# Decayed keys of a chunked delta-rule scan: transposes of scaled keys in place of products with diagonal matrices

## The chip, the cores and the metric

The kernel runs on one core of a Trainium2 chip. The metric is the device time of one execution in microseconds (us); the median of several runs is compared. A profiled execution gives the trace from which all rows below come. TensorE is called PE in the trace (its weight loads PEld), VectorE DVE, ScalarE ACT, GpSimd POOL, SyncE SP.

## The reference

A trunk of two residual layers over 512 tokens with 1024 features. Layer 0 mixes tokens by a chunked gating MLP, layer 1 by RWKV-7 time mixing; each is followed by a gated ConvFFN. The change is in the time mixing, whose core is a recurrence per head (16 heads of 64):

```python
def wkv7_scan(r, w, k, v, a, b):
    def step(state, inp):
        r_t, w_t, k_t, v_t, a_t, b_t = inp
        sa = jnp.einsum('bhvk,bhk->bhv', state, a_t)
        state = (state * w_t[:, :, None, :]
                 + sa[..., None] * b_t[:, :, None, :]
                 + v_t[..., None] * k_t[:, :, None, :])
        y_t = jnp.einsum('bhvk,bhk->bhv', state, r_t)
        return state, y_t
    ...
```

with `w` the decay, `a = -kk` and `b = kk * a_h` for normalized keys `kk`.

## The kernel before

The recurrence is done in chunks of 64 tokens (`C = 64`, `NCH = 8` chunks). Two heads share the 128 partitions (`H[0]` is partitions 0 to 63, `H[1]` 64 to 127), so there are eight pairs of heads. For each pair three generators run: `decay` (decays and their inverses; `gc` is the decay over a whole chunk, one number per feature and chunk), `operands` (`ar`: queries and `a` with decays on; `bk`: `b` and `k` with inverse decays on, 128 columns per chunk, and for the second head a copy of `b` at columns 128 to 191), and `products`, which the change edits. It does, for two groups of four chunks (`U = 4`), the products of `bk` with `ar` into the PSUM tiles `aux` (first head) and `us` (second head), masks them on VectorE into `lq`, copies the inner triangle to `ti` on ScalarE and writes `lq` to DRAM (`std`). Then it makes `bt`, the keys turned to have tokens on partitions and decayed to the end of the chunk, for which VectorE builds diagonal matrices `dg` from the identity `id2` and `gc`, and TensorE multiplies `bk` by them. `bt` goes to DRAM (`btd`), from where the scan reads it.

`acc(tag)` takes one of two PSUM buffers of a tag; the tags are `mm`, `aux`, `e` and `us`. `pairs` runs the eight pairs one after the other with the next pair's `operands` and the `decay` of the one after that between; `weave` puts steps of a `fill` generator (dense projections, `L315` to `L317` in the trace) and of `invert(0)` (inversion of the first 4 pairs' triangles: 62 small VectorE instructions, then small matmuls L1025 and L1028) between them. A scheduler below the program orders the instructions of each engine by readiness as it estimates it; engines then run their queues in that order. After the stage the scan over chunks begins (L1186 to L1213), with `invert(1)` on VectorE (from L993 on) beside it. An fp32 matmul shows as two instructions in the trace.

Lines that the text names: L853, L855, L877, L885 matmuls of `decay`; L822, L837 matmuls of the values; L1239 the transposes of the scan's results; L1188 and L1199 the scan's next steps after L1186.

Of the kernel before, what the change touches and what calls it, by code (L numbers as in the profile page):

```python
# [15 lines left out]
ALU = mybir.AluOpType  # L16
# [4 lines left out]
P = 128  # L21
# [4 lines left out]
C = 64  # L26
NCH = T // C
# [117 lines left out]
class Emit:  # L145
# [579 lines left out]
    def rwkv_main(self, r, ctx, gain):  # L725
        nc, tc, A = self.nc, self.tc, self.A
        V, S, G = nc.vector, nc.scalar, nc.gpsimd
        h0, h1 = slice(0, 64), slice(64, 128)
        H = (h0, h1)
        std, btd, vtd, rt, gc, dq = r.std, r.btd, r.vtd, r.rt, r.gc, r.dq  # L730
        U = 4
# [4 lines left out]
        def tile_(shape, tag, bufs):  # L736
            return ep.tile(shape, F32, tag=tag, bufs=bufs, name=self.uid(tag))
# [7 lines left out]
        def bc(t, n):  # L745
            return t.unsqueeze(2).to_broadcast([t.shape[0], t.shape[1], n])
# [167 lines left out]
        def products(p, u):  # L914


            g, i = divmod(p, 4)
            ar, bk = u.ar, u.bk

            dg = tile_([P, NCH, C], "dg", 1)  # L920
            V.tensor_tensor(dg, self.c("id2", C).unsqueeze(1).to_broadcast([P, NCH, C]), bc(gc[:, p], C), ALU.mult)
            masks = self.c("masks", P)

            for ch in (slice(0, U), slice(U, NCH)):
                qs = [self.acc(tag).rearrange("p (c t) -> p c t", t=P) for tag in ("aux", "us")]
                for c in range(ch.start, ch.stop):
                    for hd in range(2):
                        nc.tensor.matmul(qs[hd][:, c - ch.start, :], bk[H[hd], c, C * hd:C * hd + P], ar[H[hd], c, :],  # L928
                                         start=True, stop=True)
                lq = tile_([P, U, 2, P], "lq", 2)  # L930
                for hd in range(2):
                    V.tensor_tensor(lq[:, :, 1 - hd], qs[hd], masks.unsqueeze(1).to_broadcast([P, U, P]), ALU.mult)
                    S.copy(ti[g][H[hd], i, ch], lq[H[hd], :, 1 - hd, 0:C])
                f = lq.rearrange("p c a t -> p c (a t)")
                for hd, o, n, q in ((0, P, P, 0), (0, 2 * P, C, P + C), (1, 0, P + C, C)):
                    nc.sync.dma_start(std[g][ch, H[hd], i, o:o + n].rearrange("c p t -> p c t"), f[H[hd], :, q:q + n])
                yield
            bt = tile_([P, NCH, 2, C], "bt", BT)
            qs = [self.acc(tag).rearrange("p (c t) -> p c t", t=C) for tag in ("aux", "us")]
            for c in range(NCH):  # L940
                for hd in range(2):
                    nc.tensor.matmul(qs[hd][:, c, :], bk[H[hd], c, C * hd:C * hd + P], dg[H[hd], c, :],  # L942
                                     start=True, stop=True)
            for hd in range(2):
                S.copy(bt[:, :, hd, :], qs[hd])
            nc.sync.dma_start(btd[:, :, p].rearrange("c p a t -> p c (a t)"), bt.rearrange("p c a t -> p c (a t)"))
            yield

        def pairs():

            units = [type("Unit", (), {})() for _ in range(KT)]

            def start(p):
                if p >= KT:
                    return iter(())
                while p not in ks:
                    next(fill)
                if p == 0:
                    second_factors(p)
                return decay(p, units[p])  # L960

            yield from start(0)
            nxt = start(1)
            operands(0, units[0])
            for _ in nxt:
                yield
            for p in range(KT):
                nxt = start(p + 2)
                if p + 1 < KT:
                    operands(p + 1, units[p + 1])  # L970
                for _ in products(p, units[p]):
                    next(nxt, None)
                    yield
                done.add(p)
# [411 lines left out]
```

## Time and profile before

| | |
|---|---|
| median of 3 runs | 1292.31 us (1291.89 to 1294.6) |
| profiled execution | 1294.26 us, its span 1292.4 us |
| mean granted TensorE clock | 0.988 |
| TensorE busy | 1269.4 us (98%) |
| VectorE, ScalarE busy | 852.8 us, 631.3 us |
| stage of `products` | from about 602 to 737 us of the span |

Rows of the windows view give the stretch, its length and busy times of PE, PEld, DVE, ACT, POOL with instruction counts, then granted clock, DMA share and GB/s. Rows of the timeline give start, duration, engine, line, operation, output<-inputs, and the count when equal instructions are merged; a matmul's end is modelled, so its cost is read from the start of the next one. Rows of the groups view give the count, total busy time, mean ns of one, and idle time before them with what ended it.

### The profile page before, as it was taken

How to read it: one execution, taken by the hardware profiler on the slowest of the kernel's cores; microseconds unless marked ns; L12 is line 12 of the kernel's file. 1: busy time of each engine (PE TensorE's matmuls, PEld its weight loads, DVE VectorE, ACT ScalarE, POOL GpSimd, SP SyncE). 2: the span in 40 equal slices, each digit the busy share in tenths (PEclk: the TensorE clock that was granted, in tenths of full speed). 3: DMA queues.
4: the chain of work that ended last, by engine and by line, in shares of the span. 5: the costliest groups of instructions: out<-in, count | busy, mean ns of one | idle time of the engine just before them, and what ended most of it. 6: DMA issues, size and time to landing. Idle time of an engine off the chain costs nothing.

```text
span 1292.4 us, 19533 instructions
## 1 busy us (share of the span) xinstructions
PE 1269.4 (98%) x7591; PEld 1018.9 (79%) x7591; DVE 852.8 (66%) x1401; ACT 631.3 (49%) x1084; POOL 97.7 (8%) x119
## 2 busy tenths in 40 slices
PE   9999999999999999999999998999999999999997
PEld 6878888888888888787777776677888888888886
DVE  6465468888886444765889587765677777763233
ACT  5534456555554333565785645532544444442222
POOL 4100100000000000000000022231100000000001
PEclk9999999999999999999999998999999999999998
DMA  7332457777557764236878699764233333333332
GB/s 252 102 98 83 129 172 256 245 245 242 175 171 220 217 206 151 90 106 185 224 199 239 171 215 227 193 168 144 78 104 98 98 97 96 93 93 98 90 90 78
DMA packets 115452, 201.65 MB, mean 156 GB/s; under 512 B 21600, under 2 KB 53600, under 8 KB 115360
## 3 DMA queue, kind: packets, MB, share of 16 engines
q10 hardware_dynamic: 39104, 112.87, 29.0%
q1 hardware_dynamic: 76256, 87.54, 23.4%
q8 instruction: 59, 0.97, 0.3%
q14 instruction: 33, 0.27, 0.1%
HBM read 152.93 MB, written 47.45 MB: 155 GB/s over the span
## 4 chain that ended last, share of the span: by engine, by line
PE 88%; DVE 5%; ACT 1%; POOL 0%; issue 0%; DMA 0%; DVEq 0%; ACTq 0%; POOLq 0%
PE mm L315 10%; PE mm L316 9%; PE mm L317 9%; PE aux L315 6%; PE aux L317 6%; PE aux L316 6%; PE e L316 6%; PE e L315 6%; PE e L317 5%; PE us L317 5%; PE us L315 5%; PE us L316 5%; PE aux L928 1%; PE aux L942 1%; PE us L1186 1%; PE us L1199 1%
## 5 line engine op out<-in xcount | busy, mean ns | idle before, releaser
L234 ACT CAST w<-w 128x512 fp32r<-128x512 f32 x340 | 206.3, 610 | 374.3 <-PE aux L317 94.8
L235 DVE TENSOR_TENSOR w<-w,w 128x512 fp32r<-128x512 f32 x340 | 233.3, 688 | 196.7 <-ACT w L234 196.2
L315 PE MATMUL mm<-mxh,w 128*128 128x512 f32 (+1 forms) x416 | 171.7, 414 | 1.6 <-ACT mxh L234 1.6
L316 PE MATMUL mm<-mxl,w 128*128 128x512 f32 (+1 forms) x416 | 166.7, 401 | 0.2 <-DVE mxl L235 0.2
L317 PE MATMUL mm<-mxh,w 128*128 128x512 f32 (+1 forms) x416 | 166.3, 400 | 0.0
L342 POOL TENSOR_TENSOR ss<-ss,sq 128x512 f32<-128x512 f32 x30 | 41.0, 1368 | 777.6 <-issue 595.1
L315 PEld LDWEIGHTS mm<-mxh,w 128*128 128x128 f32 (+1 forms) x416 | 78.2, 189 | 22.0 <-issue 3.3
L317 PEld LDWEIGHTS mm<-mxh,w 128*128 128x128 f32 (+1 forms) x416 | 78.7, 189 | 18.1 <-issue 1.2
L316 PEld LDWEIGHTS mm<-mxl,w 128*128 128x128 f32 (+1 forms) x416 | 78.9, 190 | 16.3 <-issue 1.1
L539 ACT ACTIVATE cv<-z,par 128x512 f32<-128x512 f32 x88 | 71.7, 817 | 28.8 <-DVE z L537 23.8
L315 PE MATMUL us<-mxh,w 128*128 128x512 f32 x216 | 84.6, 392 | 0.0
L315 PE MATMUL aux<-mxh,w 128*128 128x512 f32 x216 | 84.5, 391 | 0.0
L317 PE MATMUL aux<-mxh,w 128*128 128x512 f32 x216 | 84.2, 390 | 0.3 <-DVE w L235 0.3
L316 PE MATMUL aux<-mxl,w 128*128 128x512 f32 x216 | 84.1, 389 | 0.0
L316 PE MATMUL us<-mxl,w 128*128 128x512 f32 x216 | 84.1, 389 | 0.0
L317 PE MATMUL us<-mxh,w 128*128 128x512 f32 x216 | 84.1, 389 | 0.0
L315 PE MATMUL e<-mxh,w 128*128 128x512 f32 x208 | 81.5, 392 | 2.5 <-ACT mxh L234 2.4
L316 PE MATMUL e<-mxl,w 128*128 128x512 f32 x208 | 81.2, 390 | 0.1
L317 PE MATMUL e<-mxh,w 128*128 128x512 f32 x208 | 81.0, 389 | 0.0
L540 DVE SCALAR_TENSOR_TENSOR cv<-z,par,cv 128x512 f32<-128x512 f32 x88 | 66.1, 752 | 19.9 <-ACT cv L539 19.9
L541 DVE SCALAR_TENSOR_TENSOR cv<-z,par,cv 128x512 f32<-128x512 f32 x88 | 66.0, 752 | 2.9
L315 PEld LDWEIGHTS e<-mxh,w 128*128 128x128 f32 x208 | 39.1, 188 | 11.3 <-ACT mxh L234 3.3
(1088 smaller groups left out, 2605.1 us busy)
## 6 DMA issues: line engine op xcount, KB each, us to landing
w<-in_wup ACTq DMA_DIRECT2D x88, 512.0 KB, 3.7
w<-in_wdn ACTq DMA_DIRECT2D x32, 512.0 KB, 3.6
st<-std SPq DMA_DIRECT2D x30, 320.0 KB, 6.9
w<-wkd ACTq DMA_DIRECT2D x16, 512.0 KB, 5.0
w<-wvd ACTq DMA_DIRECT2D x16, 512.0 KB, 5.7
w<-wod ACTq DMA_DIRECT2D x16, 512.0 KB, 4.3
w<-in_wdn ACTq DMA_DIRECT2D x16, 384.0 KB, 3.4
w<-in_wsu ACTq DMA_DIRECT2D x8, 512.0 KB, 3.7
```

What stands on the lines that cost most here:

```text
L234: nc.scalar.copy(hi[r, :n], src)
L235: (lo_eng or nc.vector).tensor_tensor(lo[r, :n], src, hi[r, :n].bitcast(F32), ALU.subtract)
L315: mm(acc, wh, xh, start=first, stop=False)
L316: mm(acc, wh, xl, start=False, stop=False)
L317: mm(acc, wl, xh, start=False, stop=last)
L342: nc.gpsimd.tensor_tensor(self.ss, self.ss, self.sq, ALU.add)
L539: nc.scalar.activation(c, z[:, 2:], AF.Identity, scale=cw(2, i), bias=self.p("conv_b", l * 44 + i))
L540: nc.vector.scalar_tensor_tensor(c, z[:, 1:T + 1], cw(1, i), c, ALU.mult, ALU.add)
L541: nc.vector.scalar_tensor_tensor(c, z[:, 0:T], cw(0, i), c, ALU.mult, ALU.add)
L928: nc.tensor.matmul(qs[hd][:, c - ch.start, :], bk[H[hd], c, C * hd:C * hd + P], ar[H[hd], c, :], start=True, stop=True)
L942: nc.tensor.matmul(qs[hd][:, c, :], bk[H[hd], c, C * hd:C * hd + P], dg[H[hd], c, :], start=True, stop=True)
L1186: nc.tensor.matmul(us[H[hd], 0, i, :], ar(i, hd, 0), vu[:, hd, i, :], start=True, stop=True)
```

## The change

`dg` goes away. `decayed` multiplies the keys `bk` of four chunks by `gc` on VectorE into `be` (one buffer), and ScalarE copies the second head's 64 columns behind them. `turned` transposes `be` on TensorE (identity `id2`), one transpose per chunk and head, into two PSUM tiles `qb` that are taken after the products of the first chunk group and held until they are copied to `bt`. The first half of the chunks is turned after the first group's products, the second half after the second group's.

```diff
-            dg = tile_([P, NCH, C], "dg", 1)
-            V.tensor_tensor(dg, self.c("id2", C).unsqueeze(1).to_broadcast([P, NCH, C]), bc(gc[:, p], C), ALU.mult)
+            id2, qb = self.c("id2", C), []
+
+            def decayed(ch):
+
+                be = tile_([P, U, 3 * C], "be", 1)
+                V.tensor_tensor(be[:, :, 0:P], bk[:, ch, 0:P], bc(gc[:, p, ch], P), ALU.mult)
+                S.copy(be[h1, :, P:], be[h1, :, 0:C])
+                return be
+
+            def turned(ch, be):
+                for c in range(U):
+                    for hd in range(2):
+                        nc.tensor.transpose(qb[hd][:, ch.start + c, :], be[H[hd], c, C * hd:C * hd + P], id2[H[hd]])
+
+            be = decayed(slice(0, U))
             masks = self.c("masks", P)
 
             for ch in (slice(0, U), slice(U, NCH)):
...
-                yield
+                if not qb:
+                    qb[:] = [self.acc(tag).rearrange("p (c t) -> p c t", t=C) for tag in ("aux", "us")]
+                    turned(ch, be)
+                    be = decayed(slice(U, NCH))
+                yield
+            turned(slice(U, NCH), be)
             bt = tile_([P, NCH, 2, C], "bt", BT)
-            qs = [self.acc(tag).rearrange("p (c t) -> p c t", t=C) for tag in ("aux", "us")]
-            for c in range(NCH):
-                for hd in range(2):
-                    nc.tensor.matmul(qs[hd][:, c, :], bk[H[hd], c, C * hd:C * hd + P], dg[H[hd], c, :],
-                                     start=True, stop=True)
             for hd in range(2):
-                S.copy(bt[:, :, hd, :], qs[hd])
+                S.copy(bt[:, :, hd, :], qb[hd])
```

The scheduler makes a new order of it. In the order of the changed kernel L931 is the transpose, L940 the product (L928 before), L1040 the second step of the inversion (L1028 before), L1198 and L1202 the scan's first matmuls (L1186 and L1190 before). A row stands for one matmul of the program, or for several if a count ends it.

TensorE, first pair, after the products of the second chunk group. Before, the products with `dg` alternate between `aux` and `us`, eight of each (the first two are shown; L877 belongs to `decay`):

```order
L316 MATMUL mm_5072<-mxl_4839,w_854_5018 128x512
L877 MATMUL e_5170<-cst,sq_5162 128x2 x4
L317 MATMUL mm_5072<-mxh_4838,w_854_5018 128x512
L942 MATMUL aux_5187<-dg_5098,bk_4984 128x64
L942 MATMUL us_5188<-dg_5098,bk_4984 128x64
```

In the changed kernel, same engine and place, the transposes of the second half of the chunks:

```order
L317 MATMUL mm_5072<-mxh_4838,w_854_5018 128x512
L931 MATMUL aux_5119<-cst,be_5129 128x64 x4
L315 MATMUL mm_5221<-mxh_4759,w_863_5073 128x512
L316 MATMUL mm_5221<-mxl_4760,w_863_5073 128x512
L317 MATMUL mm_5221<-mxh_4759,w_863_5073 128x512
L931 MATMUL us_5120<-cst,be_5129 128x64 x4
```

Four transposes of one half now stand together, with dense matmuls between them and the four of the other half.

TensorE, fifth pair, its first chunk group (the `decay` matmuls of a later pair are L877, L885, L853, L855). Before:

```order
L928 MATMUL aux_5784<-ar_5578,bk_5583 128x128
L928 MATMUL us_5785<-ar_5578,bk_5583 128x128
L928 MATMUL aux_5784<-ar_5578,bk_5583 128x128
L885 MATMUL e_5737<-cst,n_999_5693 64x128 x8
L928 MATMUL us_5785<-ar_5578,bk_5583 128x128
```

Changed:

```order
L940 MATMUL aux_5801<-ar_5590,bk_5595 128x128 x4
L940 MATMUL us_5802<-ar_5590,bk_5595 128x128 x4
L877 MATMUL e_5714<-cst,sq_5706 128x2 x4
L931 MATMUL aux_5819<-cst,be_5798 128x64 x4
L885 MATMUL e_5753<-cst,n_1005_5719 64x128 x8
L853 MATMUL e_5832<-lr_4357,l_984_5643 128x512
L855 MATMUL e_5832<-lr_4357,l_986_5645 128x512
L940 MATMUL aux_5868<-ar_5590,bk_5595 128x128
```

The products' halves no longer alternate: four of `aux`, then four of `us`; and the first of the second chunk group follows the transposes.

TensorE, from the end of the first inversion to the scan. Before, the second step of the inversion (L1028), from its second quarter to its last, has matmuls of the values (L822) and dense rows between its pieces:

```order
L1028 MATMUL aux_6489<-li_6306,tt_6309 32x32 x16
L822 MATMUL mm_6577<-cst,v_6506 128x128 x2
L1028 MATMUL aux_6559<-li_6306,tt_6309 32x32 x16
L822 MATMUL mm_6577<-cst,v_6506 128x128 x2
L315 MATMUL mm_6508<-mxh_5515,w_1107_6334 128x512
L316 MATMUL mm_6508<-mxl_5516,w_1107_6334 128x512
L317 MATMUL mm_6508<-mxh_5515,w_1107_6334 128x512
L315 MATMUL mm_6508<-mxh_5559,w_1107_6334 128x512
L316 MATMUL mm_6508<-mxl_5560,w_1107_6334 128x512
L317 MATMUL mm_6508<-mxh_5559,w_1107_6334 128x512
L1028 MATMUL aux_6559<-li_6306,tt_6309 32x32 x16
```

Changed:

```order
L1037 MATMUL aux_6441<-ix_6333,ti_4860 32x32 x31
L940 MATMUL aux_6495<-ar_6190,bk_6195 128x128 x4
L1037 MATMUL aux_6441<-ix_6333,ti_4860 32x32
L316 MATMUL mm_6550<-mxl_5680,w_1115_6364 128x512
L317 MATMUL mm_6550<-mxh_5679,w_1115_6364 128x512
L315 MATMUL mm_6550<-mxh_5731,w_1115_6364 128x512
L316 MATMUL mm_6550<-mxl_5732,w_1115_6364 128x512
L1040 MATMUL aux_6531<-li_6334,tt_6337 32x32 x32
L1040 MATMUL aux_6591<-li_6334,tt_6337 32x32 x32
L317 MATMUL mm_6550<-mxh_5731,w_1115_6364 128x512
L1198 MATMUL us_6689<-rb_6481,mxh_6476 64x64 x2
```

The last row is the scan's first. Before, twelve dense rows and L837 stand between the last L1028 and the scan's first L1186; now it is one dense row. The inversion's second step stands in one piece, and the last pair's last products (L940) stand inside its first step (L1037, which was L1025).

## The prediction

> **What bounds the kernel now.** I read the page's first section, then the windows of the stage in which the edited function runs (598 to 742 us), then the waits of TensorE there.
>
> ```profile
> PE 1269.4 (98%) x7591; PEld 1018.9 (79%) x7591; DVE 852.8 (66%) x1401; ACT 631.3 (49%) x1084; POOL 97.7 (8%) x119
> 598.00:742.00 144.00, 143.33 (x1247) 111.63 (x1247) 114.30 (x221) 96.40 (x185) 1.28 (x8) 0.97 0.76 211
> PE aux L1025 <- DVE ix L1010: 0.5, 1, 0.5
> ```
>
> The second line is the stage: length, busy time of PE, PEld, VectorE, ScalarE and GpSimd, then the granted clock. TensorE is busy for 143.33 of 144 us and waits once, for 0.5 us. So the stage ends when TensorE's queue ends: what is taken off TensorE is gained, what is put on it is lost. VectorE (114.30) and ScalarE (96.40) have some room. Behind the stage it is otherwise:
>
> ```profile
> 692.00:700.00 8.00, 8.00 (x62) 6.68 (x60) 6.58 (x16) 5.43 (x13) 0.00 (x0) 0.79 0.53 160
> 736.00:748.00 12.00, 12.00 (x130) 9.73 (x130) 1.91 (x1) 7.21 (x13) 2.36 (x4) 0.58 0.59 143
> 784.00:800.00 16.00, 12.41 (x238) 8.82 (x238) 15.07 (x34) 8.51 (x17) 4.22 (x6) 0.98 0.97 208
> ```
>
> From 784 to 800 VectorE is the full engine (15.07 of 16) and TensorE has holes of 3.6 us: there the second inversion on VectorE decides. The first two lines show the granted clock at 0.79 over 8 us and 0.58 over 12 us, behind long runs of small matmuls: 8 x 0.21 = 1.7 us and 12 x 0.42 = 5.0 us of clock lost.
>
> **The prices on TensorE.** These come from four places of the timeline. First a row of dense matmuls with one half of the products of a chunk group between them:
>
> ```profile
> 719.00 0.40 PE L315 MATMUL mm<-mxh,w 128*128 128x512 f32 x1
> 719.24 0.39 PE L316 MATMUL mm<-mxl,w 128*128 128x512 f32 x1
> 719.46 0.40 PE L317 MATMUL mm<-mxh,w 128*128 128x512 f32 x1
> 719.79 1.16 PE L928 MATMUL us<-ar,bk 64*128 64x128 f32 x8
> 720.88 0.50 PE L315 MATMUL mm<-mxh,w 128*128 128x512 f32 x1
> ```
>
> Dense matmuls start 0.23 us apart, so that is what a row costs. The eight passes of one half (four fp32 matmuls show as eight instructions) push the next dense one from 719.69 to 720.88: 1.19 us. A pass takes (1.16 - 0.27)/7 = 0.127 us, so the edge is 1.19 - 8 x 0.127 = 0.17 us. Now both halves alternating, aux from partitions 0 to 63 and us from 64 to 127:
>
> ```profile
> 611.99 0.39 PE L317 MATMUL mm<-mxh,w 128*128 128x512 f32 x1
> ...
> 613.19 0.27 PE L928 MATMUL aux<-ar,bk 64*128 64x128 f32 x1
> 613.20 0.27 PE L928 MATMUL us<-ar,bk 64*128 64x128 f32 x1
> 613.40 0.50 PE L315 MATMUL mm<-mxh,w 128*128 128x512 f32 x1
> ```
>
> Sixteen passes cost 613.40 - 611.99 - 0.23 = 1.18 us, as much as eight alone: the two halves run side by side only when they alternate in the queue. Then the products with diagonals that go away:
>
> ```profile
> L942 PE MATMUL us<-dg,bk 64*128 64x64 f32 x128 | 16.5, 275 | 0.0
> 615.47 0.48 PE L317 MATMUL mm<-mxh,w 128*128 128x512 f32 x1
> ...
> 617.61 0.27 PE L942 MATMUL us<-dg,bk 64*128 64x64 f32 x1
> 617.81 0.51 PE L315 MATMUL mm<-mxh,w 128*128 128x512 f32 x1
> ```
>
> 32 passes alternating cost 617.81 - 615.47 - 0.23 = 2.11 us for a pair of heads. Seven of the eight pairs alternate wholly or nearly; in the last the halves stand apart, some 32 x 0.127 = 4.1 us. Total: 7 x 2.11 + 4.1 = 18.9 us. The nearest thing to the new transposes:
>
> ```profile
> L1239 PE MATMUL aux<-cst,y 128*128 128x128 f32 x32 | 5.1, 283 | 0.8 <-DVE y L1235 0.8
> 773.09 0.50 PE L315 MATMUL mm<-mxh,w 128*128 128x512 f32 x1
> 773.43 0.60 PE L1239 MATMUL aux<-cst,y 128*128 128x128 f32 x4
> 773.78 0.48 PE L316 MATMUL mm<-mxl,w 128*128 128x512 f32 x1
> ```
>
> A transpose is one instruction, not two (32 for 32 in the code; the 64 products per half show as 128). Four cost 773.78 - 773.09 - 0.23 = 0.46 us, (0.60 - 0.27)/3 = 0.11 us each: a pass of a transpose is no quicker than a pass of a product.
>
> **The change, part by part.**
>
> *Products with diagonals out, transposes in.* In the new queue 13 of the 16 chunk groups have their transposes as four of one half and, later, four of the other; only three groups alternate. A half group of four costs 0.46 us by the full-height row; by the half-height row it is 4 x 0.11 plus an edge of 0.17 to 0.31, up to 0.75 us. I take 0.6 us, since the tile is 64 high as in L928, and no edge for about ten that stand beside other half-height work: 26 x 0.6 - 10 x 0.17 = 13.9. Three alternating groups at 8 x 0.055 + 0.3 = 0.74 add 2.2. Sum 16.1 against 18.9: 2.8 us gained (between 5.4 gained, at 0.46 and 0.5, and 2.8 lost, at 0.75 everywhere).
>
> [...]
>
> *Products of chunk groups.* The accumulators of the transposes are now held from the first chunk group to the end of the pair. Of two buffers for each of aux and us, one is left for the products, so the second chunk group waits for the mask multiplications of the first on VectorE. In the queue this shows as products of which the halves no longer alternate: eight groups of 16 stand apart, where before there were two (of the last pair). Each costs 2 x 1.19 - 1.18 = 1.2 us more when both halves stand alone, about 0.85 when they follow each other (16 x 0.127 - 1.18). 6 x 0.9 = 5.4 us lost (5.1 to 7.2).
>
> *VectorE and ScalarE.*
>
> ```profile
> L921 DVE TENSOR_TENSOR dg<-cst,gc 128x512 f32<-128x512 f32 x8 | 5.5, 687 | 2.9 <-PE us L942 2.9
> L933 ACT COPY ti<-lq 64x256 f32<-64x256 f32 x32 | 12.9, 403 | 10.8 <-DVE lq L932 10.4
> ```
>
> Eight products of 512 columns become sixteen: 8 x 0.69 = 5.5 us more on VectorE. Sixteen copies of 64x256 are added on ScalarE: 16 x 0.40 = 6.5 us. Their cover is the room shown above, 30 and 48 us, and the dense matmuls queued between; queued behind a scaling that waits for its one buffer is the next pair's normalization, for which TensorE would wait. I charge 0.3 us (0 to 5.5, rival D). DMAs are the same in number, size and queue; GpSimd's queue keeps its order, and in SyncE's only some writes of `lq` change places with each other.
>
> *The hand-over to the scan.* Last, the first step of the scan moves up in TensorE's queue. Before, twelve dense rows and L837 stand between the last matmul of the first inversion and L1186; after, one dense row.
>
> ```profile
> 743.72 0.80 PE L315 MATMUL mm<-mxh,w 128*128 128x512 f32 x1
> 743.84 0.58 ACT L1037 COPY ti<-aux 32x512 f32<-32x512 f32 x1 [0.94 <-PE aux L1028]
> 745.02 1.04 ACT L995 COPY ix<-ti 32x1024 f32<-32x1024 f32 x1
> 746.09 2.14 DVE L996 STREAM_TRANSPOSE li<-ix 128x1024 f32<-128x1024 f32 x1 [10.86 <-ACT ix L995]
> 749.61 0.34 PE L1186 MATMUL us<-rb,mxh 128*64 128x64 f32 x4
> 750.34 0.42 DVE L1188 COPY wt<-us 128x256 f32<-128x256 f32 x1
> ```
>
> The dense row at 743.72 is the first behind the inversion, 5.9 us ahead of L1186, in part at half clock. The second inversion begins with L996, 3.5 us ahead of L1186. After, the last products' masks and copies come only some 4 us ahead of L1186, and L996 behind them stands ahead of L1188 on VectorE. So the inversion starts about level with the scan, up to 3.5 to 4 us later against it, and the first L1199 waits about 1 us for L1188. VectorE decides at 784 to 800, so this comes out at the end but for its own idle time of that stretch. Between 0 (all absorbed) and 4, I take 2 us.
>
> *Sum.* -2.8 + 5.4 + 0.3 + 2.0 = 4.9 us. The profiled execution took 1294.26 us (span 1292.4), 1.95 above the median of 1292.31, so I add the sum to the median: 1297.2.
>
> **The rivals.**
>
> *A. The terms cancel (chance 0.24).* Half groups at 0.46 us and the later inversion absorbed: -5.4 + 5.4 + 0.3 = 0.3, so 1292.6 us. For it: the row of L1239 itself. Against it: it is a full-height tile, and half-height bursts show an edge.
>
> *B. Faster by the clock (0.15).* The last pair's products, 4.1 us of small matmuls in the run that ends in the 0.58 clock, are gone, and the transposes in their place lie between dense rows. If neither drop comes, 6.7 us are regained: 4.9 - 6.7 = -1.8; with half groups at 0.46 (3 us less) -4.8, 1287.5 us. It decides from 7.5 us below my sum on. Against it: after the change all 64 second-step matmuls of the inversion still stand in one piece just ahead of the scan's small ones, and around the fifth and the sixth pair runs of products, transposes and L877 of some 5 us form anew.
>
> *C. Slower by the clock (0.06).* If transposes keep the clock down, each further low stretch like that at 692 costs 1.7 us; two more give 1300.6. [...]
>
> *D. VectorE holds TensorE (0.10).* With one buffer left, each second chunk group waits for two mask multiplications in a queue that also carries the scalings. If each is late by one of those, 0.7 us x 8 = 5.5 us more: 1302.7. For it: this dependency is new. Against it: in the stage VectorE waited for TensorE (2.9 us at L921 alone), and TensorE for VectorE only 0.5 us.
>
> **How the numbers follow.** My own case has 0.45: 1297.2, by itself 1295 to 1300. A change within 0.2% (2.6 us) is about what a measurement cannot tell from none. Slower: 0.45 + 0.06 + 0.10 = 0.61; same: 0.24; faster: 0.15. The range reaches from 1290.5, inside B, to 1302.5, just short of D.
>
> **What the profile after would show.** Transposes as 128 instructions in place of 256, 0.11 us apart in fours; products in runs of eight of one half, at 1.19 us each. PE busy in the stage up by 2 to 4 us. L996 starting at about the time of L1186 or later, and holes of TensorE near 790 to 800 larger than 3.6 us. I am wrong if halves that follow each other overlap all the same, if a half group costs below 0.4 us, or if the clock rows at 692 and 736 go to 1.00.

## The result and the profile after

The changed kernel took 1306.4 us (median of 4 runs, 1305.61 to 1310.54) against 1292.1 for the kernel before on the same chip (1291.35 to 1294.6): a ratio of 1.0108, 95% interval 1.0092 to 1.0124. It is 14 us slower; forecast were 4.9. The profiled execution after has a span of 1304.7 us, 12.3 more than before.

Some kernels below spread over 9 to 18 us between executions, and one profile then stands for one execution, not for the median; where the profile lies at one end of the spread, that is said.

By landmarks of the two traces: the products begin 1.1 us later (603.9 against 602.8, already so before the stage), the scan 6.4 later (756.0 against 749.6), its first transposes (L1251 after, L1239 before) 12.3 later (785.7 against 773.4); from there on the distance stays. So 5.3 us are lost among the pairs and 5.9 in the first 30 us of the scan. Busy time hardly tells: TensorE is busy for 1277.4 us (before 1269.4) in 128 fewer instructions.

```profile
PE 1277.4 (98%) x7463; PEld 1018.9 (78%) x7463; DVE 858.7 (66%) x1409; ACT 638.0 (49%) x1100; POOL 97.3 (7%) x119
```

A busy row at half clock counts as busy (704 to 712 below: 8.00 of 8 us busy at a clock of 0.50). The windows view tells the two apart (length, busy PE, PEld, DVE, ACT, POOL, then the granted clock, DMA share, GB/s); first the stage by the times of before, then the places that stand out:

```profile
598.00:742.00 144.00, 140.88 (x892) 104.14 (x890) 116.02 (x224) 92.84 (x183) 1.29 (x8) 0.93 0.73 202
664.00:672.00 8.00, 7.06 (x47) 5.50 (x46) 7.00 (x13) 6.21 (x13) 0.11 (x1) 0.74 0.61 169
672.00:680.00 8.00, 8.00 (x22) 5.57 (x22) 4.44 (x8) 5.29 (x9) 0.00 (x0) 0.62 1.03 305
696.00:704.00 8.00, 6.18 (x39) 4.41 (x37) 7.40 (x17) 6.24 (x13) 0.00 (x0) 0.88 0.38 96
704.00:712.00 8.00, 8.00 (x27) 6.83 (x27) 6.42 (x16) 2.97 (x6) 0.00 (x0) 0.50 0.70 193
752.00:760.00 8.00, 5.80 (x172) 4.45 (x170) 4.29 (x6) 6.72 (x11) 2.35 (x4) 1.00 0.76 173
760.00:768.00 8.00, 7.88 (x69) 5.38 (x67) 6.35 (x21) 3.59 (x8) 1.08 (x2) 0.79 1.06 243
800.00:808.00 8.00, 4.85 (x96) 3.54 (x96) 7.14 (x16) 1.76 (x5) 3.21 (x5) 0.99 1.00 242
808.00:816.00 8.00, 7.62 (x128) 5.05 (x124) 4.59 (x9) 6.33 (x8) 1.24 (x2) 0.50 1.05 247
816.00:824.00 8.00, 7.81 (x146) 5.71 (x146) 4.89 (x10) 5.38 (x11) 2.45 (x3) 0.87 0.25 72
```

Before, at the places of the new drops and behind the second inversion:

```profile
664.00:672.00 8.00, 8.00 (x54) 5.55 (x51) 6.09 (x11) 5.17 (x10) 0.11 (x1) 1.00 0.83 236
672.00:680.00 8.00, 8.00 (x73) 6.83 (x74) 6.30 (x10) 7.88 (x13) 0.00 (x0) 1.00 0.79 209
704.00:712.00 8.00, 8.00 (x60) 6.29 (x60) 7.96 (x19) 4.94 (x12) 0.61 (x2) 1.00 0.97 291
760.00:768.00 8.00, 8.00 (x99) 5.43 (x98) 7.60 (x18) 4.98 (x10) 1.29 (x2) 1.00 1.06 270
800.00:808.00 8.00, 7.82 (x132) 5.56 (x126) 2.69 (x5) 5.67 (x9) 0.80 (x2) 0.61 0.99 219
```

The drop of the clock at 736 to 748 is gone, the one behind the second inversion (before at 800, now at 808) is longer, and three are new or larger: 664 to 680, 696 to 712 and 760. The first new one, in the timeline:

```profile
664.06 0.40 PE L317 MATMUL mm<-mxh,w 128*128 128x512 f32 x1
664.38 1.16 PE L940 MATMUL aux<-ar,bk 64*128 64x128 f32 x8
666.11 1.16 PE L940 MATMUL us<-ar,bk 64*128 64x128 f32 x8 [0.57 <-DVE lq L944]
667.20 1.28 PE L877 MATMUL e<-cst,sq 128*128 128x2 f32 x8
668.43 0.69 PE L931 MATMUL aux<-cst,be 64*128 64x64 f32 x4
669.48 1.98 PE L885 MATMUL e<-cst,n 128*64 128x128 f32 x16 [0.37 <-DVE n L880]
671.39 0.80 PE L853 MATMUL e<-lr,l 128*128 128x512 f32 x1
672.11 0.79 PE L855 MATMUL e<-lr,l 64*128 64x512 f32 x1
672.70 0.62 PE L940 MATMUL aux<-ar,bk 64*128 64x128 f32 x2
673.26 0.79 PE L315 MATMUL mm<-mxh,w 128*128 128x512 f32 x1
```

Between the dense rows at 664.06 and 673.26 stand 9.2 us of other matmuls, nearly all small (L853 and L855 of `decay`, 512 columns wide, come at the end), halves apart, with two short waits. From about L931 on matmuls take longer; the dense row behind takes 0.79 instead of 0.39. I call such a stretch a *piece*: TensorE's queue between two dense rows of the projections.

The parts are sized by windows of 4 us from 590 to 870. *Idle* is the sum of (4 - busy PE), *clock* the sum of 4 x (1 - granted clock), *ahead* the shift of the first L853 at 587, *work* what is left of the change of the span. *Apart* counts, of the 256 product passes, those in rows of four or more of one half, whatever stands between them. These are from one profile each, and *span* to *work* are differences to before, in us. *Lost, all* is not: it is the span times (1 - mean granted clock) over the whole kernel, as a mean over all executions (each clock is known to a thousandth, 1.3 us).

| kernel | median | span | ahead | idle | clock | work | apart | lost, all |
|---|---|---|---|---|---|---|---|---|
| before | 1292.1 | 1292.4 | | (6.9) | (10.2) | | 33 | 13.6 to 14.8 on four chips |
| after | 1306.4 | +12.3 | +1.1 | +4.5 | +6.8 | -0.2 | 126 | 22.2 |
| e1, keys scaled in place | 1309.7 | +14.1 | 0.0 | +9.9 | +8.5 | -4.2 | 53 | 24.3 |
| e2, diagonals, held | 1292.7 | -4.8 | -1.2 | +2.9 | -6.8 | +0.3 | 33 | 12.9 |
| e4, VectorE's columns | 1298.6 | +4.6 | +1.2 | +7.0 | +3.4 | -7.1 | 84 | 19.2 |
| e6, no scaling | 1297.2 | +1.3 | -2.2 | +9.0 | +1.7 | -7.2 | 71 | 18.7 |
| e10, products by identity | 1311.7 | +19.4 | -0.3 | +5.9 | +3.4 | +10.4 | 90 | 16.8 |
| e11, dense rows in pairs 5, 6 | 1301.0 | -0.1 | -1.4 | +2.2 | -6.8 | +5.9 | 80 | 13.3 |
| e12, TensorE's queue as after | 1305.3 | +10.5 | -1.4 | +7.0 | +5.1 | -0.2 | 126 | 20.4 |

After and e12, with the same queue on TensorE, give the same work (-0.2 twice), so that column holds to some tenths. Read: the change made TensorE's work no smaller, and added 6.8 us of lost clock and 4.5 of waiting. The last column bears the clock out beyond one profile: some 8 us more are lost than before. A us of lost clock is not quite a us of time: within the seven kernels that were executed twelve times the time rises by 0.7 to 1.0 us with it.

### The profile page after: what moved, and what is told of

Read it like the earlier page. It is cut to its first block, busy times and chain, and to the rows that moved or that the text cites. A ratio compares the mean times of both kernels' runs of the same rounds, so it can differ in the third digit from the quotient of the medians.

```text
span 1304.7 us, 19309 instructions
## 1 busy us (share of the span) xinstructions
PE 1277.4 (98%) x7463; PEld 1018.9 (78%) x7463; DVE 858.7 (66%) x1409; ACT 638.0 (49%) x1100; POOL 97.3 (7%) x119
## 4 chain that ended last, share of the span: by engine, by line
PE 87%; DVE 5%; ACT 2%; issue 1%; POOL 0%; DVEq 0%; ACTq 0%; POOLq 0%
PE mm L315 10%; PE mm L317 9%; PE mm L316 9%; PE aux L315 6%; PE aux L317 6%; PE aux L316 6%; PE e L316 5%; PE e L315 5%; PE e L317 5%; PE us L317 5%; PE us L315 5%; PE us L316 5%; PE aux L940 1%; PE e L885 1%; PE us L1198 1%; PE us L1211 1%
```

## The experiments

All kernels are made from the changed one, but for e8, e13 and e15, made from the kernel before. In brackets behind a time stand its ratio to the kernel before on the same chip and the 95% interval.

**First question: why do the halves stand apart?** The prediction blamed the accumulators that are held. e1 holds none; e2 holds them, but multiplies with diagonals; e4 moves the second head's columns from ScalarE to VectorE; e5 is e1 with e4's edit.

```diff
 e1: in the loop, instead of `be`; transposes of bk and self.acc behind the loop
+                V.tensor_tensor(bk[:, ch, 0:P], bk[:, ch, 0:P], bc(gc[:, p, ch], P), ALU.mult)
+                S.copy(bk[h1, ch, P:], bk[h1, ch, 0:C])
 e2: dg as before the change, in turned():
-                        nc.tensor.transpose(qb[hd][:, ch.start + c, :], be[...], id2[H[hd]])
+                        nc.tensor.matmul(qb[hd][:, c, :], bk[...], dg[H[hd], c, :], start=True, stop=True)
 e4 (e5 the same on bk):
-                S.copy(be[h1, :, P:], be[h1, :, 0:C])
+                V.tensor_tensor(be[h1, :, P:], bk[h1, ch, P:], bc(gc[h1, p, ch], C), ALU.mult)
```

> The same transposes and the same ScalarE copy as in the changed kernel, but the keys are scaled in place after the products of their chunk group, and both accumulators are taken only after the second group, as before the change: none is held across the groups. Before is about 1292 us, after about 1306. T1 (the accumulators held from the first chunk group keep the second group's products waiting and pull the halves apart): the loss goes, 1284 to 1293 us, and the products alternate again. T2 (the ScalarE copy of the second head's columns makes that half late, and so pulls the halves of transposes and products apart): most of the loss stays, 1296 to 1306. T3 (the added work of VectorE and ScalarE itself, which comes out at the start of the scan): the work is the same, so 1302 or more.

> The products with diagonal matrices of the kernel before, but half of the chunks at a time, with the accumulators taken after the first chunk group and held to the end of the pair, as in the changed kernel; no scaled keys and no ScalarE copy. T1 (held accumulators): 1300 to 1310 us. T2 (ScalarE copy): 1290 to 1294, as before the change. T3 (added work of VectorE and ScalarE): 1290 to 1294 too.

> The changed kernel with one instruction on another engine: the second head's columns of the scaled keys are made by a VectorE product instead of by a ScalarE copy that waits for VectorE. Accumulators held as in the changed kernel. T1 (held accumulators): 1303 to 1309 us. T2 (ScalarE copy): 1286 to 1296, with halves that alternate. T3 (added work): VectorE gets 16 more products of 64 partitions, some 0.4 us each, ScalarE loses its copies: 1302 or more if VectorE's load is what counts, about 1300 if ScalarE's is.

> Both at once: the keys scaled in place, the second head's columns by VectorE, accumulators taken after the second group and not held, transposes in one piece of 16. T1 and T2 both: 1284 to 1291 us, below the kernel before, since 128 transposes at 0.055 us a pass (alternating) replace 256 passes at 0.06. T3 (added work of VectorE): 1300 or more.

Measured: e1 1309.7 us (1.0127, 1.0108 to 1.0146), e2 1292.7 (1.0000, 0.9983 to 1.0017; profile at the low end), e4 1298.6 (1.0047, 1.0033 to 1.0062), e5 1299.6 (1.0059, 1.0039 to 1.0078; profile the fastest of twelve). By the times T1 falls twice: holding alone costs nothing (e2, 33 passes apart as before), and letting go gains nothing (e1). In e1's queue, though, the products mostly alternate again, as T1 has it (53 apart), and its work is 4 us smaller than after; it loses that and more in waiting, 3.5 us of it once for the next pair's `bk` and 2.2 for `lq`. So what sets products apart is not one edit: holding alone does not (e2), and taking away either the holding (e1) or ScalarE's copy (e4, 84) undoes a part.

For the time the copy counts, as T2 has it: with one instruction on another engine, and VectorE with more to do, e4 is 7.8 us faster than after, its work 6.9 us smaller, and e5 is 10.1 us faster than e1 by the same edit. But e1 lies above T2's range, e4 and e5 missed it, and some 6 us remain. T3, the added work itself, fits e1 and e2 and comes within 1.4 us at e4 and e5 if ScalarE's load is what counts; the copy's load and its place in the order go together in these kernels. In e4's windows VectorE (the third busy time) is nearly full or full and TensorE has holes where the clock then falls:

```profile
688.00:696.00 8.00, 7.01 (x50) 5.00 (x49) 7.80 (x20) 5.47 (x11) 0.00 (x0) 1.00 0.93 257
696.00:704.00 8.00, 6.30 (x28) 5.34 (x28) 8.00 (x20) 5.06 (x13) 0.00 (x0) 0.79 0.61 179
```

**Second question: is it VectorE?** (T4.) e6 leaves the scaling out, e7 only VectorE's part (ScalarE copies unscaled keys), e8 is the kernel before with the diagonals made twice, e9 scales on GpSimd.

```diff
 e6: decayed() returns bk[:, ch]
 e7:
-                V.tensor_tensor(be[:, :, 0:P], ...)
-                S.copy(be[h1, :, P:], be[h1, :, 0:C])
+                S.copy(be[h1, :, C:], bk[h1, ch, C:])
 e8:
+            V.tensor_tensor(dg, self.c("id2", C)..., bc(gc[:, p], C), ALU.mult)
 e9:
+                G.tensor_tensor(be[:, :, 0:P], bk[:, ch, 0:P], bc(gc[:, p, ch], P), ALU.mult)
+                G.tensor_tensor(be[h1, :, P:], bk[h1, ch, P:], bc(gc[h1, p, ch], C), ALU.mult)
```

> The changed kernel without the scaling: the transposes read the undecayed keys, so the 16 VectorE products and the 16 ScalarE copies are left out, and the diagonals too (the decay is missing from the output). Placement and held accumulators are the same; halves alternate. What is left is what the change does on TensorE alone. T4 (VectorE is full from about 640 to 664 and from 688 to 712 us, so that what TensorE waits for comes late, and behind each hole the clock falls; ScalarE's copy adds the split halves): TensorE gains about 6 us by the transposes and VectorE has 5.5 us less to do than before the change: 1282 to 1288 us. If instead the transposes themselves bring the clock down: 1292 or more.

> The scaling left out on VectorE, but a ScalarE copy of the second head's columns (64 x 512, some 0.6 us) kept in front of the transposes; the first head's transposes read the undecayed keys (the decay is missing from the output). VectorE has less to do than before the change, ScalarE some 10 us more, and transposes of the two heads stand apart in the queue as in the changed kernel. T4 with VectorE as the cause: 1283 to 1290 us. If ScalarE's copy and the split halves are the cause by themselves: 1296 or more.

> The kernel before, with its diagonals made twice by VectorE: 8 x 0.69 = 5.5 us more on VectorE, as the change adds, and nothing else. T4 (VectorE's full stretches): 1296 to 1301 us. If VectorE's room covers it, as the prediction took it: 1291 to 1294.

> The changed kernel with the scaling and the second head's columns made by GpSimd, which is idle in this stage (its product of 128 x 512 took 1.37 us elsewhere); VectorE has 5.5 us less to do than before the change and ScalarE has no copies. Halves alternate. T4: 1283 to 1290 us, faster than both kernels. If GpSimd's 2 us per group come too late for the transposes, or if it slows VectorE by working beside it: 1293 or more.

Measured: e6 1297.2 (1.0037, 1.0025 to 1.0049), e7 1304.9 (1.0094, 1.0081 to 1.0107), e8 1304.1 (1.0072, 1.0048 to 1.0095; 1290.3 to 1308.6, profile at the low end), e9 1307.0 (1.0114, 1.0096 to 1.0132; profile at the high end). T4 as stated falls: with nothing added on VectorE or ScalarE and 7.2 us less work on TensorE, e6 is still slower than before. And e7, with no scaling on VectorE at all, loses nearly as much as the changed kernel: ScalarE's copy (here 64x512) makes it 7.7 us slower than e6, the third pair in which that copy costs 8 to 10 us. Where e6's gain goes is in its trace: the scan begins 140.3 us behind the first product (146.8 before), but from there to its first transposes take 33.4 us (23.8 before). The first row of its waits of TensorE (total, times, longest), then its windows there:

```profile
PE us L1195 <- DMA vu<-vtd: 4.0, 1, 4.0
```

```profile
744.00:752.00 8.00, 5.50 (x64) 4.13 (x64) 6.82 (x21) 4.89 (x12) 1.24 (x2) 1.00 1.06 242
752.00:760.00 8.00, 6.16 (x54) 4.66 (x55) 1.59 (x4) 0.36 (x1) 0.00 (x0) 0.57 1.06 237
```

TensorE waits 4.0 us for the values' DMA, and behind the hole the clock is 0.57 for 8 us. So a shorter stage is not a shorter kernel here. Yet e8 shows that VectorE's 5.5 us are not covered either: added to the kernel before, with no transposes at all, they cost 9 us by the ratio. They cost it by the clock in the main: the three executions with a mean clock of 0.991 or more took 1290.3 to 1296.6 us, the seven with 0.980 or less 1304.0 to 1308.6. Its one profile, at 1294, does not show at which places. e7 and e9 differ from their models in TensorE's queue too, and both have long pieces; in e9's profile 13.5 us of waiting and 11.9 of lost clock are added and 8.7 us of work are gone.

**Third question: is it the kind of matmul, or the piece?** Over the eighteen profiles from 590 to 870 us (dense rows that an experiment adds end a piece too): of the pieces of 8 us and more, 27 of 27 have a drop of the clock that begins between 1.5 us behind their start and 2 us behind their end; of 6.5 to 8 us 5 of 12; of 4 to 6.5 us 14 of 96; of 2.5 to 4 us 6 of 231. Before has two pieces over 8 us (at 732 and 790, each at an inversion), after has three (at 664, 696 and 801). That is T5. It doesn't tell small matmuls from waits: in all but three of the 57 drops TensorE also had idle time (0.05 to 2.6 us) in the 3.4 us ahead. e10 has products by the identity in place of the transposes; e11 puts dense rows into the pairs whose pieces are long.

```diff
 e10:
-                        nc.tensor.transpose(qb[hd][:, ch.start + c, :], be[...], id2[H[hd]])
+                        nc.tensor.matmul(qb[hd][:, ch.start + c, :], be[...], id2[H[hd]], start=True, stop=True)
 e11: on both accumulators ahead of each group's products and of the first transposes, if p in (4, 5):
+                        for _ in range(2):
+                            nc.tensor.matmul(q, r.lr[0][:, 0:P], r.lr[0], start=True, stop=True)
```

> The changed kernel with products by the identity in place of the transposes: same scaled keys, same ScalarE copies, same placement; 256 passes instead of 128, some 6 us more work on TensorE. The scheduler, which estimates them as longer, also lets more halves alternate, and fewer long pieces of the queue are without dense rows. T5 (what costs is the clock and the holes behind runs of TensorE without dense matmuls; the transposes are only small matmuls like the others): decided by the queue, not by the kind: 1296 to 1304 us. T6 (the transposes themselves don't count as work for the clock): the drops of the clock at 664 to 680 and 700 to 712 us go away, 1292 to 1297. Neither (cost of the passes alone): 1306 + 6 = 1312.

> The changed kernel with dense matmuls added: in the fifth and the sixth pair, two 128 x 512 matmuls (their results are overwritten at once) into each accumulator ahead of the products and ahead of the transposes, 24 in all, 24 x 0.23 = 5.5 us more work on TensorE at full clock. The long pieces without dense rows at 664 to 673 and 696 to 707 us are broken up. T5: two of the four drops of the clock go away or get shorter, 2 x 3.4 to 5 us: 1301 to 1306 in spite of the added work. T6, or if the clock follows VectorE's lateness only: 1309 to 1313.

Measured: e10 1311.7 us (1.0127, 1.0105 to 1.0150; profile the slowest of six); e11 1301.0 (1.0052, 1.0035 to 1.0069; profile at the low end). e10 has the time of "cost of the passes alone", not its parts: its work is 10.6 us more than after and 3.4 us less clock is lost. T6 isn't needed: with no transpose in it, a piece of 9.3 us at 668 brings half clock (672 to 683). The drop at 702 is gone, but so is the long piece there. e11 is 5.4 us *faster* than after, though its 24 rows are work: 5.9 us more work than before against -0.2. In its profiled execution, the timeline of the fifth pair (L937 are the added rows, L948 the products):

```profile
661.84 0.72 PE L937 MATMUL aux<-lr 128*128 128x512 f32 x2
662.49 1.16 PE L948 MATMUL aux<-ar,bk 64*128 64x128 f32 x8
663.64 0.73 PE L937 MATMUL us<-lr 128*128 128x512 f32 x2
664.31 0.93 PE L948 MATMUL us<-ar,bk 64*128 64x128 f32 x6
665.17 1.05 PE L877 MATMUL e<-cst,sq 128*128 128x2 f32 x8
...
667.62 1.09 PE L885 MATMUL e<-cst,n 128*64 128x128 f32 x16
```

and the windows of e11 at both places:

```profile
664.00:672.00 8.00, 8.00 (x54) 5.84 (x53) 6.83 (x13) 6.75 (x15) 0.11 (x1) 1.00 0.68 163
672.00:680.00 8.00, 8.00 (x54) 5.89 (x53) 6.01 (x10) 7.54 (x11) 0.00 (x0) 1.00 0.92 296
696.00:704.00 8.00, 8.00 (x69) 6.67 (x66) 7.15 (x18) 5.84 (x14) 0.00 (x0) 1.00 0.59 167
```

The clock stays at 1.00 and L885 takes 1.09 us, not 1.98. Over all executions 13.3 us of clock are lost against 22.2 after, so the gain is in the clock, and not in this one execution alone.

e13 does the same ahead of the eight pieces of the two inversions in the kernel before; e15 and e16 are controls of e11.

```diff
 e13: in invert(), on each of the four accumulators
+                        nc.tensor.matmul(ps, cb[:, 0:P], cb, start=True, stop=True)   # twice, cb is bf16
 e15: e11's rows in the kernel before, with p in (4, 5);   e16: e11 with p in (1, 2)
```

> The kernel before with two dense matmuls (bf16, 128 x 512, overwritten at once) ahead of each of the eight pieces of the two inversions' small matmuls, 16 x 0.23 = 3.7 us more work on TensorE. Before, the clock is at half for some 10 us behind the first inversion's run (736 to 748) and for 8 us behind the second's (798 to 806), together 8 us lost. T5: one or both drops go or get shorter: 1284 to 1291 us. If dense rows there don't hold the clock: 1294 to 1297.

> Control: the same 24 dense matmuls in the fifth and sixth pair of the kernel before (ahead of both chunk groups and of the products with diagonals), 5.5 us more work on TensorE. Before, there is one drop of the clock in that place, 2.7 us lost (690 to 704). T5: what is gained there is at most that, so 1292.5 + 5.5 - 2.7 = 1295 to 1298. If dense rows help for some other reason (an order that suits the queue everywhere): 1287 to 1292, below the kernel before.

> Control: the changed kernel with the same 24 dense matmuls in the second and third pair (615 to 650 us), where no drop of the clock stands; the long pieces without dense rows in the fifth and sixth pair stay, though the order there is not the same to the instruction. T5: the added work comes out in full, 1309 to 1313. If dense rows help wherever they stand: 1299 to 1304, as with those in the fifth and sixth pair.

Measured: e13 1294.0 us (1.0000, 0.9987 to 1.0014), e15 1292.0 (0.9990, 0.9978 to 1.0001; profile the slowest of twelve), e16 1303.8 (1.0087, 1.0071 to 1.0102). None is what T5 expected. (The drop that bounds e15's forecast loses 1.7 us by the trace, not 2.7.) In e13's profile the drop behind the first inversion is gone, but the one at 692 stays, one at 722 is new, and the one at 794 is longer: as much is lost as before (10.2). e16 is 2.6 us faster than after, with overlapping intervals, though its rows are 5.5 us of work and stand where no drop was; in its profile the fifth pair's piece is gone all the same, because the scheduler, with other times ahead, ordered that place otherwise; the sixth pair's (8.7 us) is there, with its drop. In e15 no product passes stand apart any more (33 before), and its work is 0.8 us *smaller* in spite of the rows. So rows of this kind act through the whole order, not only at their place; what e11 shows is that the clock holds where pieces are broken up (their waits are gone too); how much of its gain comes from its own two places, and how much from the order elsewhere, stays open.

**Fourth question: the scan's start.** After, ScalarE makes the scaled block `wb` behind copies of the inversions, and TensorE waits for it. From the timeline of the changed kernel, all engines mixed, rows left out:

```profile
756.69 1.04 ACT L1007 COPY ix<-ti 32x1024 f32<-32x1024 f32 x1
757.76 1.16 ACT L1049 COPY ti<-aux 32x512 f32<-32x512 f32 x2
757.77 2.04 DVE L1008 STREAM_TRANSPOSE li<-ix 128x1024 f32<-128x1024 f32 x1 [3.01 <-ACT ix L1007]
758.93 0.40 ACT L835 ACTIVATE wb<-cst,par 128x128 f32<-128x128 f32 x1
759.39 1.48 PE L837 MATMUL mm<-rt,wb 128*128 128x512 f32 x2 [2.19 <-ACT wb L835]
759.65 0.44 DVE L1200 COPY wt<-us 128x256 f32<-128x256 f32 x1
```

```diff
 e12: the two lines that make wb, ahead of `while m not in done: yield`
 e17:
-            S.activation(wb, self.c("bones", P), AF.Copy, scale=self.p("r_k", m))
+            G.tensor_tensor(wb, self.c("bones", P), self.p("r_k", m).to_broadcast([P, P]), ALU.mult)
```

> The changed kernel with one ScalarE instruction moved: the scaled block of ones that the matmul of the values reads is made before its generator waits for the pair, so it no longer stands behind the inversion's copies in ScalarE's queue at the scan's start; TensorE's queue is the same to the instruction. The wait of 2.2 us at the scan's start (757 to 759) goes. If that wait decides: 1303.5 to 1304.5 us, and more if the drop of the clock at 757 to 764 goes with it (1301 to 1303). If VectorE's second inversion decides there: 1306.

> The changed kernel with the scaled block of ones of the values made by GpSimd instead of ScalarE, so that it stands behind no copies of the inversion; TensorE's queue changes in places from the sixth pair on. The wait of 2.2 us at the scan's start goes. If that wait decides: 1303 to 1305; with the drop of the clock at 757 to 764 gone too: 1300 to 1303. If it comes back as a wait on the values' DMA or on VectorE: 1306.

Measured: e12 1305.3 us (1.0089, 1.0072 to 1.0106), e17 1304.5 (1.0092, 1.0076 to 1.0107; profile the fastest of six). e12 missed its purpose: in its trace TensorE waits 2.2 us for `wb` as before, because ScalarE's queue still has it behind the copies; it tells nothing of the wait. In e17 the wait is gone and so is the drop at 760, but others take most of its place in its waits of TensorE:

```profile
PE us L1211 <- issue: 1.5, 1, 1.5
PE us L1198 <- DMA vu<-vtd: 0.9, 1, 0.9
```

From the scan's start to its first transposes it takes 28.5 us, against 29.7 after and 23.8 before: the wait was worth 1.2 to 1.9 us, which the overlapping intervals of e17 and after can't tell from nothing. The larger part of the 5.9 us stays open.

**Together.** e14 joins e4's, e11's and e17's edits.

> Three edits of the changed kernel together, to see whether it can beat the kernel before: the 24 dense matmuls in the fifth and sixth pair, the second head's columns by VectorE (1298.6 us alone), and the scaled block of ones of the values by GpSimd. If the parts add: 1298.6 - 5 - 2 = about 1291 to 1293; if the drops of the clock that the two edits remove are the same ones: 1296 to 1299.

Measured: 1297.1 us (1.0024, 1.0009 to 1.0040; 1289.0 to 1300.0). The parts don't add; no version tried beats the kernel before by more than can be measured (e15, at 1292.0, is the nearest).

## Why the prediction was right or wrong

*Direction right, size 9 us short.* The sign was in part luck: of the 4.9 us forecast, 2.6 were work on TensorE, which came out at -0.2. Of the 12.3 us that the profile lost, waiting took 4.5 (forecast 2.3), lost clock 6.8 (forecast 0), and 1.1 were there ahead of the stage. By terms:

- *Transposes, 2.8 us gained.* Mis-sized, on the safe side. A half group of four costs 617.45 - 616.74 - 0.23 = 0.48 us, at the low end of 0.46 to 0.75:

```profile
616.74 0.39 PE L317 MATMUL mm<-mxh,w 128*128 128x512 f32 x1
617.05 0.46 PE L931 MATMUL aux<-cst,be 64*128 64x64 f32 x4
617.45 0.50 PE L315 MATMUL mm<-mxh,w 128*128 128x512 f32 x1
...
644.30 0.40 PE L317 MATMUL mm<-mxh,w 128*128 128x512 f32 x1
...
645.02 0.50 PE L315 MATMUL mm<-mxh,w 128*128 128x512 f32 x1
```

  An alternating group of eight costs 0.49, where I took 0.74. By these prices 26 x 0.48 + 3 x 0.49 = 14.0, a gain of 4.9.
- *Products whose halves stand apart, 5.4 us lost.* About right in size: 126 - 33 = 93 passes more apart are some six groups of 16, as forecast, and the work of e4, which has 84 apart and more than half of whose transposes alternate, is 6.9 us smaller. The cause named was half of it at most: the held accumulators alone set none apart (e2), and ScalarE's copy, behind which the scheduler sets one half after the other, has its part in it (e4); it was priced only as load. Together the two terms gave -0.2, not +2.6.
- *VectorE and ScalarE, 0.3 us.* Wrong step: I took their cover from the mean of the stage (30 and 48 us of room). VectorE was full for stretches of it (before, 7.96 of the 8 us from 704 to 712), and in e8 its 5.5 us alone cost 9, mostly in clock. ScalarE's copy, part of the same 0.3, cost 8 to 10 us in three pairs of kernels, in two of them chiefly as more work on TensorE (6.9 us between after and e4, 5.5 between e7 and e6). In the changed kernel TensorE waits at 702 for a scaling (1.7 us), with the clock then at half.
- *The hand-over to the scan, 2 us.* Direction right, too small, and not by the mechanism given. L1008 starts at 757.77, 1.7 us behind the first L1198, as forecast, and L1211 waits 1.0 us for `wt`. But 2.2 us of waiting come from ScalarE's queue, which is in no term, and a drop of the clock follows. The holes near 800 grew only from 3.0 to 3.2 us (5.03 and 4.85 busy of 8).
- *The clock, 0 in the sum.* The step that failed. Rival B said that the drop at 736 goes; it did. Rival C priced two more at 1.7 us each, with a chance of 0.06; what came were two at 5 us. Its condition, that transposes keep the clock down, no run shows (in e10 a piece without a transpose brings half clock for 10.2 us). I had quoted both drops of before as standing "behind long runs of small matmuls" and had seen in the new queue that in the fifth and sixth pair such runs "of some 5 us form anew", but priced them at nothing; with halves apart and waits inside they took 9.2 and 10.3 us. Where ScalarE's copy is left out (e4, e5, e6), the clock is most of what remains: 3.9 to 6.4 us more of it lost than before, in kernels that take 4.5 to 7.2 us longer.
- *Rival D* (VectorE holds TensorE): the time it gave, 1302.7, is nearer, but the row that tells, waits of TensorE for `lq`, shows one of 0.6 us, not eight of 0.7.

## What to carry to other kernels

Before pricing a change to TensorE's small matmuls, list the pieces of its queue without dense rows, before and after, with the waits inside: here every piece of 8 us or more (27 of 27) brought a drop of the clock, worth 1.7 to 6.8 us each. Room on an engine must be read from the stretch where the new work lands, not from a stage's mean. And where a scheduler orders the queues, one copy on another engine can reorder many others (here it cost 8 to 10 us); look at what the new queue lets alternate, and measure with more than one execution, since the clock differs between them (e8: a mean of 0.978 to 0.994 over twelve executions).

## What was unexpected of the hardware

The granted clock can fall while the trace has TensorE busy without a hole. The kernel before, at the end of the pairs (the clock falls at 738.0):

```profile
732.00:736.00 4.00, 4.00 (x66) 3.89 (x65) 2.06 (x3) 2.43 (x5) 0.00 (x0) 1.00 0.65 183
736.00:740.00 4.00, 4.00 (x83) 3.71 (x82) 0.00 (x0) 2.11 (x4) 0.00 (x0) 0.75 0.45 116
```

It does so three times in the eighteen profiles; the other 54 drops have some idle time close ahead. Each drop is to 0.50 and lasts 3.41, 6.83, 10.24 or 13.65 us, so 1.7, 3.4, 5.1 or 6.8 us are lost: multiples of one length. Their starts fit one grid, too: in the changed kernel 667.87, 702.01, 760.03 and 807.82 us, that is 10, 17 and 14 lengths of (807.82 - 667.87)/41 = 3.413 us apart. Why 19 of the 108 pieces of 4 to 8 us have a drop and the others none is not shown. For the drops here transposes are not needed (e10: half clock from 672 to 683 in and behind a piece without one); whether they add to them no run shows.

Two halves of four transposes cost no more in alternation than one half alone (0.49 and 0.48 us after), the same as was seen of the products (1.18 and 1.19 before).
